# A two-layer hybrid block on one core: warm-up zeros in a place of their own, a fourth load buffer that comes in later, and a first block whose seven-product part starts four units later

## The chip, the cores and the metric

The kernel runs on one core of one Trainium2 chip. The metric is the time on the device in microseconds (us) of one execution; a kernel is run several times and the median counts. A profile is one further execution, recorded by the hardware profiler. Times inside it are counted from the start of its span. The engines are named as in the profile: PE multiplies matrices (PEld loads its weights), DVE and ACT work on vectors, POOL is hardly used, and SP issues the loads from memory (DMA). Each engine works through its own list of instructions in order. An instruction that waits holds up all that stand behind it on its engine.

## The reference

`x` has 256 rows of 2048 numbers in fp32. Two layers follow each other; each is a mixer and a gated feed-forward part (FFN), both added to the stream `h`, and a last norm ends it.

```python
def swiglu(hn, w_gate, w_up, w_down):
    return (jax.nn.silu(hn @ w_gate) * (hn @ w_up)) @ w_down

def reference(x, ...):
    h = x
    for layer in range(DEPTH):
        j = layer // 2
        if layer % 2 == 0:
            h = h + gdn_rglru_mixer(rmsnorm(h, ab_norm[j]), ab_w_in[j], ...)
        else:
            h = h + fox_moba_mixer(rmsnorm(h, cd_norm[j]), cd_w_in[j], ...)
        h = h + swiglu(rmsnorm(h, ffn_norm[layer]), ffn_w_gate[layer], ffn_w_up[layer], ffn_w_down[layer])
    return rmsnorm(h, final_norm)
```

The first mixer joins a gated delta rule and a linear recurrence, the second two kinds of attention. Most of the work is products of `hn` (256 x 2048) with weights: D_FF is 5632, so one FFN reads 3 x 2048 x 5632 weights.

## The kernel before

**Precision and units.** Every large product keeps fp32 by a split: a weight block `raw` of 128 x 1024 is loaded (`load`, L161), ACT rounds it to `whi` (L174), DVE forms `wlo` = raw - whi (L175), and PE makes three products: x-high with whi, x-high with wlo, x-low with whi (L366, L367, L368 in the FFN; L229 to L231 and L197 to L199 in the first mixer; L268 to L270 elsewhere). One such block is called a unit here. The activations stand transposed in `X`, high and low part. There are three buffers for `raw`, four for `whi`, three for `wlo`. Inside an FFN a fourth buffer `raw4` takes every fourth load; it lies in the pool `mx`, whose memory belonged to the mixer before, so that its first load must wait until the last readers and writers of that memory are done. The count of loads (`loads`) runs through the whole program.

**The start.** PE first multiplies a tile of zeros, `wz`, into `Pz` (L90), eleven times; each of these fp32 products is two rows of the trace. `wz` lies in a pool of its own that is closed at once, so the next pool to open gets its place: that is `xt`, the transposed input, in four quarters (L211). `first` then computes the first three weight columns (q, k, v of head 0): per quarter, ACT makes X high (L221) and DVE X low (L222) for four k, ACT and DVE split three half-size weight blocks (L225, L226), and PE makes 36 products of 256 columns, 144 in all. `x` in its untransposed form is loaded into `h` in four pieces (L893); ACT squares each (`junk`, L281), and DVE makes the row norms from the sums (`rstd`, L299 to L103), among the splits of the units of head 1 (`wstat`, L197).

**The FFN.** Gate and up weights are done in 11 blocks of 512 columns (`block`), for both of them and both row halves t. The 16 k-slices fall into four quarters m. Quarters 1 to 3 are plain: 12 units, named p0 to p11 here, of 12 products of 512 columns each, and each goes to the two banks of its matrix. Quarter 0 (2 x 2 sub-matrices b11, b12, b22, b21) is done by a scheme with seven products instead of eight, the generator `seven`: it loads b11, b12, b22, b21, forms the sums T1 = b11 + b12, T3 = b12 + b22, T2 = T1 + b22, T4 = T2 + b21 on DVE (`total`, L337), splits each sum (`thi` on ACT L340, `tlo` on DVE L341), and PE makes 6 products for each of seven steps. The sums of activations that it needs are made once, by `combine` (L349 to L354). A table of counts decides how many steps follow each plain unit:

```python
        lead, trail = 2, 3 if nd > 3 else 2
        gaps = max(len(plain) - lead - trail, 1)
...
            while k < len(sevens) and k < (j - lead + 2) * len(sevens) // gaps:
                next(sevens[k])
```

With these numbers one step follows each of the units p1 to p7. In the first block of an FFN `combine` runs ahead of p1 (`hooks[1]`), and `rstd` ahead of p8. The stream into the FFN comes from the mixer's last product: DVE adds it to h (L321), ACT squares it (`junk`), PE transposes it (`Pt`, L290), ACT and DVE write the last quarter of X (L291, L292).

**The order.** The program text gives what is done; a scheduler places the instructions on each engine, so a row of an engine's list need not stand where the text has it. The loads all go through SP's one list.

Of the kernel before, what the change touches and what calls it, by code (L numbers as in the profile page):

```python
# [4 lines left out]
F32, F32R, I32 = dt.float32, dt.float32r, dt.int32  # L5
AF = mybir.ActivationFunctionType
# [41 lines left out]
def body(tc, A, out):  # L48
    nc = tc.nc
    PE, S, V, G = nc.tensor, nc.scalar, nc.vector, nc.gpsimd  # L50
# [4 lines left out]
    cst = pool("cst", 1)  # L55
# [7 lines left out]
    loads, more = [0], []  # L63

    def phase(mixer):

        st = ExitStack()
        sub = lambda name, bufs: st.enter_context(tc.tile_pool(name=name, bufs=bufs))
        ogp.pool = sub("og" if mixer else "hid", 3 if mixer else 1)
        mx.pool = sub("mx" if mixer else "fx", 1)  # L70
        more[:] = [] if mixer else [1]
        return st

    def ms(shape, name):
        return msp.tile(shape, F32, tag="ms", name=name)
# [3 lines left out]
    X = res.tile([128, NK, 2, T], F32R, name="X", tag="X")  # L79
# [1 line left out]
    col = cst.tile([128, NCOL], F32, name="col")  # L81
    nc.sync.dma_start(col[:, 0:16], A["col"][:, 0:16])

    with tc.tile_pool(name="warm", bufs=1) as wp:
        wz = wp.tile([128, 256], F32, name="wz")
        V.memset(wz, 0.0)
        S.activation(wz[:, 0:1], wz[:, 1:2], AF.Copy)
        Pz = ms([128, 256], "Pz")
        for _ in range(11):
            PE.matmul(Pz, wz[:, 128:256], wz[:, 0:256], start=True, stop=True)  # L90
    tb = {n: tab[:, a:b] for n, (a, b) in TAB.items()}
    cl = {n: col[:, a:b] for n, (a, b) in COL.items()}

# [67 lines left out]
    def load(src):  # L161

        loads[0] += 1
        if more and loads[0] % 4 == 0:
            raw = mx.tile([128, 1024], F32, name="raw4", tag="raw4", bufs=1)
        else:
            raw = wr.tile([128, 1024], F32, name="raw")
        nc.sync.dma_start(raw, src)
        return raw
# [198 lines left out]
                PE.matmul(self.t, xl, hi[:, kk], start=False, stop=kk == 1 and self.i == self.n - 1)  # L368
            self.i += 1

    def block(src, x, comb, nd, hooks, tail=0):

# [41 lines left out]
            return [[c1, w5], [v, w7]]  # L416

        sevens = [s for m in comb for s in [seven(m)] for _ in range(7)]
        lead, trail = 2, 3 if nd > 3 else 2
        gaps = max(len(plain) - lead - trail, 1)  # L420
        held, e, k = [], None, 0
        for j, (i, u) in enumerate(plain):
# [14 lines left out]
            while k < len(sevens) and k < (j - lead + 2) * len(sevens) // gaps:  # L437
                next(sevens[k])
                k += 1
                if k == len(sevens):  # L440
                    e = ends()
        return [[y.t for y in f] for f in F], e

    def ffn(L, then, fin=None):

        gu, dn = A[f"gu{L}"], A[f"dn{L}"]
# [11 lines left out]
        b = 0  # L458
        for piece in (4, 4, 3):
            hid = ogp.tile([128, 16, 2, T], F32R, name="hid", tag="hid")  # L460
            for j in range(piece):
                hooks = {2: turn, 3: turn} if todo else {}
                if b == 0:
                    hooks[1] = lambda: cx.update({0: combine(X[:, 0:4])})
                    hooks[8] = rstd
                if j == 1:
                    hooks[5] = lambda: ch.update({0: combine(hid[:, 0:4])})
                F, e = block(lambda i, u: gu[b, u, i], lambda k: X[:, k], {0: lambda: cx[0]}, 4, hooks)
                a = [mx.tile([128, 512], F32, name=f"fa{t}", tag="fa", bufs=4) for t in range(2)]
                for t in range(2):  # L470
                    r = nrm["rs"][:, t:t + 1]
                    V.tensor_tensor(out=a[t], in0=F[t][0], in1=e[t][0], op=(ALU.add, ALU.subtract)[t])
                    S.activation(a[t], a[t], AF.Silu, scale=r)
                for t in range(2):
                    r = nrm["rs"][:, t:t + 1]
                    V.tensor_tensor(out=e[t][1], in0=F[t][1], in1=e[t][1], op=ALU.add)
                    V.scalar_tensor_tensor(out=a[t], in0=e[t][1], scalar=r, in1=a[t], op0=ALU.mult, op1=ALU.mult)
                    todo.append((hid, j, t, a[t]))
                b += 1
# [691 lines left out]
```

## Time and profile before

| | |
|---|---|
| time, median of 3 runs | 2288.99 us (2286.92 to 2289.01) |
| profiled execution, its own time | 2286.04 us |
| its span | 2284.2 us |
| PE busy | 2259.0 us, 99% of the span |
| DVE busy | 1805.0 us, 79% |
| ACT busy | 1205.9 us, 53% |
| moved from memory | 418.22 MB, 185 GB/s on average |
| mean granted clock of PE | 0.996 |

The profiled execution's own time is 1.8 us longer than its span, which begins with the first instruction and ends with the last. It lies 2.95 us under the median of the runs. The granted clock is a share of full speed, 1.00 for 2.4 GHz and 0.50 for 1.2 GHz. A busy PE is not a PE at its best: matmuls overlap, so what counts is how often one starts.

### The profile page before, as it was taken

The numbers are of one execution on the slowest core, as the hardware profiler recorded it, in microseconds if no ns is written. First come the engines' busy times: TensorE is split into PE (matmuls) and PEld (weight loads), VectorE is DVE, ScalarE is ACT, GpSimd is POOL, SyncE is SP. The second block draws the span as 40 slices with busy tenths as digits, with TensorE's granted clock in tenths as the row PEclk, the third lists the DMA queues.
The fourth block names the chain that finished last, engine by engine and source line by source line (L and its number), as shares of the span: only waits on it lengthen the run. The fifth ranks groups of instructions, "written<-read, shape, count | busy, mean of one in ns | idle before, by whom it ended". The sixth has DMA issues, their size and how long they took to land.

```text
span 2284.2 us, 31143 instructions
## 1 busy us (share of the span) xinstructions
PE 2259.0 (99%) x11620; PEld 1906.7 (83%) x11620; DVE 1805.0 (79%) x2655; ACT 1205.9 (53%) x1580; POOL 2.0 (0%) x6
## 2 busy tenths in 40 slices
PE   8999999999999999999999999999999999999997
PEld 8999888788888888888878888887888888888886
DVE  6898676688887888888976658857888788787888
ACT  6765654554554554454654444445554455554554
POOL 0000000000000000000000000000000000000000
PEclk9999999999999999999999999999999999999999
DMA  7444445566565566566554455455565565566564
GB/s 244 148 161 155 145 154 181 167 203 201 185 204 202 188 208 192 191 200 201 185 169 166 151 172 168 166 191 179 186 208 194 192 205 197 183 206 204 186 213 147
DMA packets 118647, 422.35 MB, mean 185 GB/s; under 512 B 13248, under 2 KB 14784, under 8 KB 118368
## 3 DMA queue, kind: packets, MB, share of 16 engines
q1 hardware_dynamic: 118208, 419.84, 55.4%
q8 instruction: 91, 1.49, 0.3%
q10 hardware_dynamic: 288, 0.52, 0.1%
q14 instruction: 60, 0.49, 0.1%
HBM read 418.22 MB, written 2.10 MB: 184 GB/s over the span
## 4 chain that ended last, share of the span: by engine, by line
PE 97%; DVE 1%; DMA 1%; ACT 1%; issue 0%; DVEq 0%; ACTq 0%; SPq 0%
PE F L366 17%; PE F L368 17%; PE F L367 17%; PE Pw L194 7%; PE Pw L199 6%; PE Px L268 5%; PE Px L270 4%; PE Px L269 4%; PE M L367 3%; PE M L368 3%; PE M L366 3%; PE Pw L197 2%; PE Pw L198 2%; PE Ph L453 1%; PE Psc L975 1%; DVE wlo L175 0%
## 5 line engine op out<-in xcount | busy, mean ns | idle before, releaser
L174 ACT CAST whi<-raw 128x1024 fp32r<-128x1024 f32 x744 | 779.9, 1052 | 889.1 <-PE F L368 424.1
L175 DVE TENSOR_TENSOR wlo<-raw,whi 128x1024 fp32r<-128x1024 f32 x744 | 906.1, 1222 | 329.5 <-PE F L367 141.9
L366 PE MATMUL F<-whi,X 128*128 128x512 f32 x1100 | 432.2, 393 | 5.6 <-ACT whi L174 5.6
L368 PE MATMUL F<-whi,X 128*128 128x512 f32 x1100 | 429.6, 391 | 0.0
L367 PE MATMUL F<-wlo,X 128*128 128x512 f32 x1100 | 429.4, 390 | 0.0
L199 PE MATMUL Pw<-X,wlo 128*128 128x256 f32 x1104 | 310.2, 281 | 0.0
L366 PEld LDWEIGHTS F<-whi,X 128*128 128x128 f32 x1100 | 206.8, 188 | 48.7 <-ACT whi L174 7.1
L368 PEld LDWEIGHTS F<-whi,X 128*128 128x128 f32 x1100 | 207.2, 188 | 43.6
L367 PEld LDWEIGHTS F<-wlo,X 128*128 128x128 f32 x1100 | 207.5, 189 | 42.1
L194 PE MATMUL Pw<-X,whi 128*128 128x512 f32 x640 | 230.2, 403 | 0.0
L366 PE MATMUL F<-whi,hid 128*128 128x512 f32 x536 | 209.9, 392 | 0.0
L199 PEld LDWEIGHTS Pw<-X,wlo 128*128 128x128 f32 x1104 | 209.5, 190 | 0.2
L368 PE MATMUL F<-whi,hid 128*128 128x512 f32 x536 | 208.7, 389 | 0.0
L367 PE MATMUL F<-wlo,hid 128*128 128x512 f32 x536 | 208.6, 389 | 0.0
L341 DVE TENSOR_TENSOR tlo<-T,thi 128x1024 fp32r<-128x1024 f32 x136 | 165.4, 1221 | 19.8 <-ACT thi L340 19.6
L340 ACT CAST thi<-T 128x1024 fp32r<-128x1024 f32 x136 | 142.7, 1049 | 28.8 <-PE M L368 14.9
L194 PEld LDWEIGHTS Pw<-X,whi 128*128 128x128 f32 x640 | 120.2, 188 | 29.4 <-issue 0.7
L197 PE MATMUL Pw<-X,whi 128*128 128x256 f32 x464 | 135.0, 291 | 0.0
L198 PE MATMUL Pw<-X,whi 128*128 128x256 f32 x464 | 131.4, 283 | 0.0
L368 PEld LDWEIGHTS F<-whi,hid 128*128 128x128 f32 x536 | 100.6, 188 | 21.0
L367 PEld LDWEIGHTS F<-wlo,hid 128*128 128x128 f32 x536 | 100.7, 188 | 20.6
L366 PEld LDWEIGHTS F<-whi,hid 128*128 128x128 f32 x536 | 100.6, 188 | 20.3
(372 smaller groups left out, 3241.9 us busy)
## 6 DMA issues: line engine op xcount, KB each, us to landing
raw<-in_gu SPq DMA_DIRECT2D x352, 512.0 KB, 4.1
raw<-in_dn SPq DMA_DIRECT2D x176, 512.0 KB, 4.2
raw<-in_w0w SPq DMA_DIRECT2D x74, 512.0 KB, 3.6
raw<-in_wo SPq DMA_DIRECT2D x64, 512.0 KB, 3.5
raw<-in_w1w SPq DMA_DIRECT2D x64, 512.0 KB, 3.5
raw<-in_w1x SPq DMA_DIRECT2D x32, 512.0 KB, 3.5
raw<-in_w0x SPq DMA_DIRECT2D x16, 512.0 KB, 3.5
raw<-in_w0w SPq DMA_DIRECT2D x12, 256.0 KB, 5.3
```

What stands on the lines that cost most here:

```text
L174: S.copy(hi, raw)
L175: V.tensor_sub(lo, raw, hi.bitcast(F32))
L194: PE.matmul(P.rearrange("p a b -> p (a b)"), hi[:, kk], X[:, k].rearrange("p a b -> p (a b)"), start=k == 0, stop=False)
L197: PE.matmul(P[:, 0], hi[:, kk], X[:, k, 0], start=k == 0, stop=False)
L198: PE.matmul(P[:, 0], hi[:, kk], X[:, k, 1], start=False, stop=False)
L199: PE.matmul(P[:, 0], lo[:, kk], X[:, k, 0], start=False, stop=k == NK - 1)
L268: PE.matmul(Ps[t], x[:, 0, ts], hi[:, kk], start=k == 0, stop=False)
L340: S.copy(hi, t)
L341: V.tensor_sub(lo, t, hi.bitcast(F32))
L366: PE.matmul(self.t, xh, hi[:, kk], start=self.i == kk == 0, stop=False)
L367: PE.matmul(self.t, xh, lo[:, kk], start=False, stop=False)
L368: PE.matmul(self.t, xl, hi[:, kk], start=False, stop=kk == 1 and self.i == self.n - 1)
```

## The change

Three things are changed. The zeros `wz` get a place in the pool of constants, which nobody else uses, and they are multiplied six times instead of eleven. `loads` is set to -12 whenever a stage (mixer or FFN) begins, and `raw4` is used only at positive multiples of four, that is from the 16th load of a stage on. In the first block of each FFN `combine` runs ahead of p4 instead of p1, and `lead` is 5 instead of 2: with 4 gaps in place of 7, one step of the seven follows p4, two follow p5, two p6 and two p7.

```diff
@@ -69,6 +69,7 @@
         ogp.pool = sub("og" if mixer else "hid", 3 if mixer else 1)
         mx.pool = sub("mx" if mixer else "fx", 1)
         more[:] = [] if mixer else [1]
+        loads[0] = -12
         return st
 
     def ms(shape, name):
@@ -81,13 +82,12 @@
     col = cst.tile([128, NCOL], F32, name="col")
     nc.sync.dma_start(col[:, 0:16], A["col"][:, 0:16])
 
-    with tc.tile_pool(name="warm", bufs=1) as wp:
-        wz = wp.tile([128, 256], F32, name="wz")
-        V.memset(wz, 0.0)
-        S.activation(wz[:, 0:1], wz[:, 1:2], AF.Copy)
-        Pz = ms([128, 256], "Pz")
-        for _ in range(11):
-            PE.matmul(Pz, wz[:, 128:256], wz[:, 0:256], start=True, stop=True)
+    wz = cst.tile([128, 256], F32, name="wz")
+    V.memset(wz, 0.0)
+    S.activation(wz[:, 0:1], wz[:, 1:2], AF.Copy)
+    Pz = ms([128, 256], "Pz")
+    for _ in range(6):
+        PE.matmul(Pz, wz[:, 128:256], wz[:, 0:256], start=True, stop=True)
     tb = {n: tab[:, a:b] for n, (a, b) in TAB.items()}
     cl = {n: col[:, a:b] for n, (a, b) in COL.items()}
 
@@ -161,7 +161,7 @@
     def load(src):
 
         loads[0] += 1
-        if more and loads[0] % 4 == 0:
+        if more and loads[0] > 0 and loads[0] % 4 == 0:
             raw = mx.tile([128, 1024], F32, name="raw4", tag="raw4", bufs=1)
         else:
             raw = wr.tile([128, 1024], F32, name="raw")
@@ -368,7 +368,7 @@
-    def block(src, x, comb, nd, hooks, tail=0):
+    def block(src, x, comb, nd, hooks, tail=0, lead=2):
@@ -416,7 +416,7 @@
         sevens = [s for m in comb for s in [seven(m)] for _ in range(7)]
-        lead, trail = 2, 3 if nd > 3 else 2
+        trail = 3 if nd > 3 else 2
         gaps = max(len(plain) - lead - trail, 1)
@@ -461,11 +461,11 @@
                 if b == 0:
-                    hooks[1] = lambda: cx.update({0: combine(X[:, 0:4])})
+                    hooks[4] = lambda: cx.update({0: combine(X[:, 0:4])})
                     hooks[8] = rstd
-                F, e = block(lambda i, u: gu[b, u, i], lambda k: X[:, k], {0: lambda: cx[0]}, 4, hooks)
+                F, e = block(lambda i, u: gu[b, u, i], lambda k: X[:, k], {0: lambda: cx[0]}, 4, hooks, lead=2 if b else 5)
```

What the change does to the engines' lists is shown at three places. First SP, at the start of the program, with what each load waits for in brackets (names with DMAHW are earlier loads); before:

```order
L82 DMA col<-in_col 128x16
L216 DMA raw<-in_w0w 128x512 x3
L218 DMA tab<-in_tab 128x152
L219 DMA col<-in_col 128x233
L216 DMA raw<-in_w0w 128x512 x2
L216 DMA raw<-in_w0w 128x512 [waits DMAHW0_49]
L893 DMA h<-in_x 128x2x512 [waits DMAHW1_49]
L211 DMA xt<-in_xt 128x1024 [waits DMAHW2_49,PE_49,Activation_49]
```

And now:

```order
L83 DMA col<-in_col 128x16
L211 DMA xt<-in_xt 128x1024
L216 DMA raw<-in_w0w 128x512 x3
L218 DMA tab<-in_tab 128x152
L219 DMA col<-in_col 128x233
L211 DMA xt<-in_xt 128x1024
L216 DMA raw<-in_w0w 128x512 [waits DMAHW0_49]
L216 DMA raw<-in_w0w 128x512 [waits DMAHW1_49]
L216 DMA raw<-in_w0w 128x512 [waits DMAHW2_49]
L211 DMA xt<-in_xt 128x1024 [waits DMAHW3_49]
L211 DMA xt<-in_xt 128x1024 [waits DMAHW4_49]
```

The first quarter of `xt` moved to second place and waits for nothing; the first piece of h went behind all quarters and weight halves of `first`.

Second SP again, at the beginning of the first FFN (the second FFN has the same rows under other numbers). Before, 5147 is p0's block, 5175 p1's, 5193 b11, 5223 b12, 5255 b22:

```order
L168 DMA raw_5147<-in_gu0 128x1024 [waits DMAHW0_49,DVE_49,Activation_49]
L168 DMA raw_5193<-in_gu0 128x1024 [waits DMAHW1_49,DVE_49]
L168 DMA raw_5205<-in_gu0 128x1024 [waits DMAHW2_49,DVE_49]
L168 DMA raw_5223<-in_gu0 128x1024 [waits DMAHW3_49,DVE_49]
L168 DMA raw4_5175<-in_gu0 128x1024 [waits PE_49,Activation_49,Pool_49]
L168 DMA raw4_5237<-in_gu0 128x1024 [waits DMAHW7_49,DVE_49]
L168 DMA raw_5255<-in_gu0 128x1024 [waits DMAHW4_49,DVE_49]
```

Now 5138, 5156, 5174, 5192 and 5220 are p0 to p4, 5238 is b11, 5250 p5, 5268 b12, 5282 b22, 5294 p6, 5336 p7, 5354 b21, and 5457 is p11, the 16th load:

```order
L168 DMA raw_5138<-in_gu0 128x1024 [waits DMAHW0_49,DVE_49,Activation_49]
L168 DMA raw_5156<-in_gu0 128x1024 [waits DMAHW1_49,DVE_49]
L168 DMA raw_5174<-in_gu0 128x1024 [waits DMAHW2_49,DVE_49]
L168 DMA raw_5192<-in_gu0 128x1024 [waits DMAHW3_49,DVE_49]
L168 DMA raw_5220<-in_gu0 128x1024 [waits DMAHW4_49,DVE_49,Activation_49]
L168 DMA raw_5238<-in_gu0 128x1024 [waits DMAHW5_49,DVE_49]
L168 DMA raw4_5457<-in_gu0 128x1024 [waits PE_49,Activation_49,Pool_49]
L168 DMA raw_5250<-in_gu0 128x1024 [waits DMAHW6_49,DVE_49]
L168 DMA raw_5268<-in_gu0 128x1024 [waits DMAHW7_49,DVE_49]
L168 DMA raw_5282<-in_gu0 128x1024 [waits DMAHW2_49,DVE_49]
L168 DMA raw_5294<-in_gu0 128x1024 [waits DMAHW0_49,DVE_49]
```

The load that waits for the mixer's memory moved from fifth place, where p1's block hung on it, to seventh, where p11's does.

Third DVE in the same block, from T1 on; before:

```order
L337 TENSOR_TENSOR T1_5225<-raw_5193,raw_5223 128x1024
L352 TENSOR_TENSOR cc4_5166<-cf_5165,cc4_5166 128x256
L175 TENSOR_TENSOR wlo_5178<-raw4_5175,whi_5177 128x1024
L352 TENSOR_TENSOR cc4_5166<-cf_5165,cc4_5166 128x256
L175 TENSOR_TENSOR wlo_5196<-raw_5193,whi_5195 128x1024
L175 TENSOR_TENSOR wlo_5208<-raw_5205,whi_5207 128x1024
L354 TENSOR_TENSOR comb_5167<-cc4_5166,comb_5167 128x1024
L341 TENSOR_TENSOR tlo_5228<-T1_5225,thi_5227 128x1024
L175 TENSOR_TENSOR wlo_5240<-raw4_5237,whi_5239 128x1024
L337 TENSOR_TENSOR T3_5285<-raw_5223,raw_5255 128x1024
```

Now:

```order
L101 TENSOR_TENSOR rt_5388<-rs_5389 128x2
L102 SCALAR_TENSOR_TENSOR rt_5388<-rt_5388,rx_5387 128x2
L175 TENSOR_TENSOR wlo_5253<-raw_5250,whi_5252 128x1024
L354 TENSOR_TENSOR comb_5212<-cc4_5211,comb_5212 128x1024
L337 TENSOR_TENSOR T1_5270<-raw_5238,raw_5268 128x1024
L103 SCALAR_TENSOR_TENSOR rs_5389<-rt_5388,rs_5389 128x2
L101 TENSOR_TENSOR rt_5388<-rs_5389 128x2
L102 SCALAR_TENSOR_TENSOR rt_5388<-rt_5388,rx_5387 128x2
L103 SCALAR_TENSOR_TENSOR rs_5389<-rt_5388,rs_5389 128x2
L337 TENSOR_TENSOR T3_5312<-raw_5268,raw_5282 128x1024
L341 TENSOR_TENSOR tlo_5273<-T1_5270,thi_5272 128x1024
```

T1 moved from the start of the block to behind p5's split, the small operations of `rstd` (L299 to L103) came up from behind the seven steps, and T3 now stands ahead of T1's `tlo`, where before it stood behind it.

## Rows read from the trace of the kernel before

**Rows 1.** The page: the span, and PE's busy time.

```profile
span 2284.2 us, 31143 instructions
PE 2259.0 (99%) x11620; PEld 1906.7 (83%) x11620; DVE 1805.0 (79%) x2655; ACT 1205.9 (53%) x1580; POOL 2.0 (0%) x6
```

**Rows 2.** PE's waits: in total us, how often, longest us.

```profile
PE F L366 <- ACT whi L174: 5.6, 4, 2.5
PE Pw L229 <- ACT X L221: 4.5, 1, 4.5
```

**Rows 3.** Timeline of the start: start us, length us, engine, [idle before, releaser].

```profile
1.19 1.36 SPq L216 DMA_DIRECT2D raw<-in_w0w  x3
2.28 7.86 PE L90 MATMUL Pz<-wz 128*128 128x256 f32 x22 [2.28 <-ACT wz L87]
10.23 1.29 SPq L211 DMA_DIRECT2D xt<-in_xt  x3
14.04 4.91 ACT L221 ACTIVATE X<-xt,col 128x256 fp32r<-128x256 f32 x12 [2.45 <-DMA xt<-in_xt]
14.60 0.56 PE L229 MATMUL Pw<-X,whi 128*128 128x256 f32 x2 [4.46 <-ACT X L221]
...
24.82 2.50 DVE L226 TENSOR_TENSOR wlo<-raw,whi 128x512 fp32r<-128x512 f32 x4
...
33.65 0.28 PE L197 MATMUL Pw<-X,whi 128*128 128x256 f32 x1
```

**Rows 4.** SP's waits: the load of xt.

```profile
SPq L211 <- PE Pz L90: 4.5, 1, 4.5
```

**Rows 5.** Windows at the start, PE alone, the last of all engines: busy, clock, DMA, GB/s.

```profile
2.28:7.55 5.27, 5.27 (x12) 1.00 0.96 301
14.60:18.30 3.70, 3.70 (x17) 0.54 0.99 361
18.30:33.64 15.34, 15.34 (x129) 1.00 0.89 319
15.00:20.00 5.00, 5.00 (x30) 4.88 (x30) 4.47 (x12) 4.46 (x11) 0.00 (x0) 0.67 0.99 367
```

**Rows 6.** Windows of PE in FFN blocks: the first, second, first again, half clock.

```profile
444.22:492.64 48.42, 45.36 (x195) 0.96 0.57 186
492.64:535.79 43.15, 43.15 (x195) 1.00 0.60 196
1559.14:1607.77 48.63, 45.67 (x195) 0.96 0.56 186
451.80:455.20 3.40, 3.03 (x8) 0.50 0.59 175
```

**Rows 7.** The chain that ended last, where the FFNs begin.

```profile
444.46 1.41 ACT junk L281 x4
445.93 3.45 DMA raw<-in_gu
...
1560.81 3.37 DMA raw<-in_gu
```

**Rows 8.** PE's timeline in the first FFN block.

```profile
450.57 0.73 PE L366 MATMUL F<-whi,X 128*128 128x512 f32 x2 [2.47 <-ACT whi L174]
```

**Rows 9.** DVE's timeline in the first FFN block.

```profile
467.54 2.35 DVE L175 TENSOR_TENSOR wlo<-raw,whi 128x1024 fp32r<-128x1024 f32 x2
469.81 1.22 DVE L337 TENSOR_TENSOR T<-T,raw 128x1024 f32<-128x1024 f32 x1
470.94 0.16 DVE L98 TENSOR_SCALAR rs<-rt 128x2 int32<-128x2 int32 x1
471.14 0.16 DVE L101 TENSOR_TENSOR rt<-rs 128x2 f32<-128x2 f32 x1
```

**Rows 10.** DVE's timeline where the first norms are made.

```profile
29.56 0.16 DVE L299 TENSOR_REDUCE rx<-ssp 128x2 f32<-128x8 f32 x1 [2.23 <-ACT junk L281]
35.92 1.22 DVE L175 TENSOR_TENSOR wlo<-raw,whi 128x1024 fp32r<-128x1024 f32 x1
```

## The prediction

> **What bounds the kernel now.** I read the page first. PE is busy for 2259.0 of the 2284.2 us [rows 1], so only stretches in which PE idles or runs slowly can give time back. PE's waits then name the places: 4.5 us before its first real product, and 5.6 us in four waits for a `whi` in the FFNs [rows 2]. The other engines wait for PE almost everywhere else, so what they do matters only where PE waits for them.
>
> The timeline of the start shows the first place. PE multiplies zeros from 2.28 for 7.86 us, and only then, at 10.23, does SP issue the loads of xt; the first real product starts at 14.60 [rows 3]. SP's waits say why: the load of xt waited 4.5 us for Pz [rows 4], because it lies where the zeros lay. After the idle stretch PE's clock is half: 17 products take 3.70 us, while the 129 that follow take 15.34 us, 0.119 each [rows 5]. Product 145 of the real work starts at 33.65 [rows 3], and from there on PE runs without a gap to the FFN.
>
> The second place is the first block of each FFN. The second block takes 43.15 us, the first 48.42 and in the second FFN 48.63, with as many products [rows 6]. So each first block loses 5.27 and 5.48 us. The chain shows the cause: the mixer's last ACT work on h, then a load of 3.45 us (3.37 in the second FFN) that could not be issued before [rows 7]. PE stood 2.47 us [rows 8], and the clock fell to half for the stretch 451.80 to 455.20 [rows 6].
>
> **The change, part by part: the start.** xt is now SP's second load; that place is issued at 1.19 [rows 3]. From issue to the first X took 3.8 us before (10.23 to 14.04), so the first X starts at about 5.0. Four X on ACT at 0.41 each (4.91 / 12), then the first half-size `whi` at about 0.6, end at 7.2. Six zero products are twelve rows, which took until 7.55 [rows 5]; so the first real product starts at about 7.6, and its `wlo` is there about 8.2. I add 0.6 us for this and for a last stretch at half clock, and 144 times 0.119 = 17.1: the 144 end at 25.3 instead of 33.65, a gain of 8.35.
>
> Does the feed hold this pace? A quarter is 36 products, 4.3 us of PE. DVE needs four X at 0.41 and three `wlo` at 0.63 (2.50 / 4 [rows 3]), 3.5 us; ACT is alike. The loads of a quarter are 0.52 + 3 x 0.26 = 1.31 MB, 3.6 us at the 367 GB/s of [rows 5]. All three stay under PE, with some 0.7 us per quarter to spare.
>
> What is late next is h. All of its four pieces stand behind `first`'s loads, so they land at about the time of before: 2.1 MB of h, 1.0 MB of two units and 5.4 MB ahead of them make 8.5 MB, 23 us at 367 GB/s, after about 3 us until the first lands: 26.2. Two squares of 0.7 later, at 27.6, DVE starts the norms (29.56 before [rows 10]); about 14 small steps that depend on each other, 0.20 each [rows 9], and two of 128 columns end at 30.8. On DVE the third `wlo` of head 1 stands behind them and is ready at 32.0. PE wants it after two units of 24 products, 25.3 + 5.8, and one small product of the norms: 31.5. I take a wait of 0.5, which leaves **-7.8 us**. Bounds: no wait, -8.4; or the norms come as late as before, the third `wlo` at 35.92 + 1.22 = 37.1 [rows 10], a wait of 5.6, and only -2.7. I stay near the first, since the loads before h lose the stretch in which the queue waited for Pz.
>
> The five zero products that are gone lay ahead of an idle stretch before; now they would lie ahead of real work, and the 7.6 above counts that. The place for wz and the order inside the mixer I cost at nothing: PE is the engine waited for there. Blocks after the first keep four load buffers in rotation, only beginning elsewhere in it, so their loads wait for the same uses as before: nothing either, and 2 us of disturbance per FFN would be the bound if this were wrong.
>
> **The first FFN blocks.** Four plain units no longer hang on the late load: p0 to p4 have their blocks in the three ordinary buffers. The 5.27 and 5.48 us go away. But the seven steps now come compressed and with three buffers. I count from the block's first product. PE, without waits: a unit of 12 products is 2.72 us (0.227 each: 43.15 less 0.9 for eight transposes, over 186), a step of six 1.36; with 0.8 for the transposes p0 ends at 3.5, p1 6.3, p2 9.0, p3 11.7, p4 14.4, step b11 15.8, p5 18.5, and then the six products of T1 start.
>
> DVE: p5's `wlo` needs the place of p3's, free at 11.7, and stands behind eight small steps of `rstd`, which run until about 12.1. A DVE operation of 128 x 1024 starts 1.14 us after the one before and lasts 1.22 [rows 9]. So p5's `wlo` is done at 13.2, the last part of `combine` at 14.4, T1 at 15.6. Only then can b22 be loaded, as its buffer is the one that T1 read b11 from: 15.6 + 3.45 [rows 7] = 19.05. T3 needs b22 and stands ahead of T1's `tlo` on DVE: T3 until 20.2, `tlo` until 21.4. PE wanted it at 18.7: **a wait of 2.7 us**.
>
> The same repeats with b21, whose buffer is b22's, last read by T2. After T3 DVE does T1's `tlo`, two `wlo`, T3's `tlo` and T2, 5 x 1.14, until 25.9; the load lands at 29.4; T4 until 30.6, and behind it T2's `tlo` until 31.8. PE has 35 products from 21.4 on, 7.95 us, and stands at 29.4: **a second wait of 2.45 us**. The 72 products that are left take 16.35, and the block ends at 48.2. Against 48.42 and 48.63 that is -0.2 and -0.4: the stall is not removed but moved.
>
> Half clock changes this little. If the first wait brings it, as 2.47 us did [rows 8], eight products start in 3.40 us [rows 6] where fifteen would, 1.6 us lost; PE then comes 1.6 later to the second wait, which shrinks as much, since DVE's chain sets its end. Bounds for a block: neither wait, -5.3; both, with half clock after the second instead, +1.4. The prices of DVE and of the load are rows of the same kind in the same stage, so I take the sum.
>
> [...]
>
> **Sum.** -7.8 - 0.2 - 0.4 = -8.4 us. The profiled execution's own time, 2286.04, becomes 2277.6; it lay 2.95 under the median, so I put the same difference on the median: 2288.99 - 8.4 = **2280.6 us**.
>
> **Rivals.** (B) *The waits of the first block do not appear, or half of them.* For it: T1 needs only be 2.7 us earlier, or DVE might find `rstd` done in pauses. Against it: T3 stands ahead of `tlo` in DVE's list, and the buffer rule holds whatever the clock does. It gives -7.8 - 10.7 = -18.5, 2270.5; with half the waits about 2275.5.
>
> (C) *h takes the gain of the start back.* The norms come as late as before, a wait of 5.6 where I have 0.5; or the two FFN blocks end 1.4 later by half clock after the second wait. The first gives 2288.99 - 2.7 - 0.6 = 2285.7, the second 2288.99 - 7.8 + 2.8 = 2284.
>
> (D) *PE's clock does not rise in `first`* and the kernel ends slower. The place is the first 144 products; before, eleven zero products ran ahead of an idle stretch, and half clock lasted for 17 products after it. If fewer zeros and pauses between the first products keep the clock at half, 144 products take 144 x 3.70 / 17 = 31.3 us, from 7.6 to 38.9 instead of 33.65: +5.3 - 0.6 = +4.7, 2293.7. Each us at half clock costs half a us, so the start gives nothing back once about 16 us run so. Against it: before, real products brought the clock up after 17 of them [rows 5].
>
> On (D) the Trainium skill, TensorE: Matmul & The Clock Gate, "What's actually happening", says that "the default state is throttled, and activity releases the throttle". By that rule five zeros fewer speak for (D), the earlier real products against it; the trace agrees as far as the half clock behind the idle stretch goes.
>
> **How the numbers follow.** The forecast, within about 3 us either way, has 0.55; (B) 0.20, (C) 0.17, (D) 0.06, and 0.02 is left for something slower still. The range from 2274 to 2287 takes in the half of (B) and all of (C). About 0.2% (4.6 us) is what a measurement of this kernel can tell from no change. The forecast is faster by more than that except for its slow edge; (B) is faster; (C) is the same or just at the bound; (D) is slower or at the bound. So faster 0.75, same 0.19, slower 0.06.
>
> **What would show it.** In the profile after: no wait of SP's xt load for Pz, a first real product near 7.6, and head 1's first product near 25.3, at full clock from about 8 on. In the FFNs no wait for `whi` at the block's start, but two waits for `tlo`, at L367 of an M bank, some 18.7 and 29.4 us into the first block, and a block length of about 48. First blocks of 43 to 46 us would make (B) right; PE waiting for the third `wlo` of head 1 for several us, (C); a granted clock of 0.5 beyond the first 10 us, (D).

## The result, and the profile of the changed kernel

The changed kernel takes **2272.97 us** (median of 6 runs, 2272.34 to 2276.77). The kernel before, run beside it, takes 2287.14 (6 runs, 2285.41 to 2289.01). The ratio is 0.9941 with a 95% interval of 0.9931 to 0.9952, about 14.2 us less. The forecast was 8.4 us less and 2280.6, with a range down to 2274.0. The sign was right. The gain was larger than every case but rival (B), and the median lies 1.0 us below the range.

The page, its span and PE's busy time, for comparison with [rows 1]:

```profile
span 2270.7 us, 31138 instructions
PE 2252.9 (99%) x11610; PEld 1901.3 (84%) x11610; DVE 1804.5 (79%) x2655; ACT 1201.8 (53%) x1579; POOL 2.0 (0%) x6
```

The span is 13.5 us shorter. This profiled execution took 2272.64 us in all, close to its median, while that of before lay 1.1 under its median of six; the rest of the 14.2 is there. PE's waits, in total us, how often, longest us, which answer to [rows 2]:

```profile
PE M L367 <- DVE tlo L341: 1.7, 4, 0.5
PE Pw L199 <- DVE wlo L175: 1.1, 2, 0.8
PE Prb L311 <- PE Pw L199: 0.8, 1, 0.8
PE Pw L197 <- ACT whi L174: 0.6, 1, 0.6
```

Beside these stands PE's first wait of 2.3 us for `wz`, which the kernel before has too. Both rows of [rows 2] are gone: PE no longer waits 5.6 us for a `whi` in the FFNs nor 4.5 us for X. New are three rows at the start (`Pw` L199, `Prb`, `Pw` L197). The four waits for a `tlo` are the places where the forecast had two waits of 2.7 and 2.45 us per block; the longest is 0.5.

The timeline of the start (start us, length us, engine, and in brackets the idle time before and what ended it), for [rows 3]:

```profile
1.19 0.42 SPq L211 DMA_DIRECT2D xt<-in_xt  x1
2.28 5.49 PE L90 MATMUL Pz<-wz 128*128 128x256 f32 x12 [2.28 <-ACT wz L87]
5.42 1.70 ACT L221 ACTIVATE X<-xt,col 128x256 fp32r<-128x256 f32 x4 [3.19 <-DMA xt<-in_xt]
7.69 0.49 PE L229 MATMUL Pw<-X,whi 128*128 128x256 f32 x1
...
12.57 2.96 SPq L216 DMA_DIRECT2D raw<-in_w0w  x6
...
24.98 0.28 PE L229 MATMUL Pw<-X,whi 128*128 128x256 f32 x1
...
26.09 0.39 PE L197 MATMUL Pw<-X,whi 128*128 128x256 f32 x1 [0.59 <-ACT whi L174]
27.35 0.39 PE L199 MATMUL Pw<-X,wlo 128*128 128x256 f32 x1 [0.76 <-DVE wlo L175]
33.95 0.46 PE L311 MATMUL Prb<-dg,tab 128*128 128x128 f32 x2 [0.83 <-PE Pw L199]
35.24 0.39 PE L199 MATMUL Pw<-X,wlo 128*128 128x256 f32 x1 [0.36 <-DVE wlo L175]
```

`first` went as forecast: its first product at 7.69 (forecast 7.6), its last ones right behind 24.98, where the kernel before stood at 33.3. Head 1's first product comes at 26.09 (25.3) instead of 33.65. But then PE waits four times, 0.59 + 0.76 + 0.83 + 0.36 = 2.54 us, where the forecast had one wait of 0.5. At the FFN's first product 4.75 us are left of the 7.56 (439.47 against 444.22).

The windows of the first block of the first FFN and of the second (busy time of PE, PEld, DVE, ACT, POOL, then clock, DMA share, GB/s):

```profile
439.47:484.42 44.95, 44.12 (x196) 35.38 (x194) 38.99 (x55) 26.54 (x32) 0.00 (x0) 1.00 0.62 198
1550.63:1595.29 44.66, 43.79 (x195) 35.46 (x194) 39.03 (x55) 26.54 (x32) 0.00 (x0) 1.00 0.63 200
```

The first blocks last 44.95 and 44.66 us, 3.5 and 4.0 less than in [rows 6], and nothing in them runs at half clock. The forecast was 48.2. So 13.5 us of span are 4.75 at the start, 3.47 and 3.97 in the two first blocks, and 1.3 in the rest: 0.35 and 0.7 in the later blocks of the two FFNs, 0.3 behind the last product, and nothing in the second mixer.

Why the waits for `tlo` are short is seen on DVE and SP in the first block (the T at 453.95 is T1, at 456.49 T3, at 462.99 T2; the `wlo` at 451.67 is p5's, at 460.71 p6's):

```profile
451.67 1.23 DVE L175 TENSOR_TENSOR wlo<-raw,whi 128x1024 fp32r<-128x1024 f32 x1
453.95 1.22 DVE L337 TENSOR_TENSOR T<-raw 128x1024 f32<-128x1024 f32 x1
456.49 1.22 DVE L337 TENSOR_TENSOR T<-raw 128x1024 f32<-128x1024 f32 x1 [0.66 <-DMA raw<-in_gu]
457.63 1.22 DVE L341 TENSOR_TENSOR tlo<-T,thi 128x1024 fp32r<-128x1024 f32 x1
460.71 1.23 DVE L175 TENSOR_TENSOR wlo<-raw,whi 128x1024 fp32r<-128x1024 f32 x1 [0.72 <-ACT whi L174]
462.99 1.22 DVE L337 TENSOR_TENSOR T<-T,raw 128x1024 f32<-128x1024 f32 x1
...
452.93 0.33 SPq L168 DMA_DIRECT2D raw<-in_gu  x1
455.20 0.33 SPq L168 DMA_DIRECT2D raw<-in_gu  x1
461.96 0.33 SPq L168 DMA_DIRECT2D raw<-in_gu  x1
```

T1 ends at 455.17, 15.7 us into the block, as forecast (15.6). But b22 is not loaded behind it. Its load is issued at 452.93, right behind p5's `wlo` (451.67 + 1.23 = 452.90), into the place that p5's block has just left. The load that waits for T1 (455.20) is p6's. T3 starts at 456.49 and T1's `tlo` ends at 458.85, where the forecast had 439.47 + 21.4 = 460.9. b21 is issued at 461.96, behind p6's `wlo` (460.71 + 1.23 = 461.94), not behind T2, which ends at 464.21.

### The profile page after: what moved, and what is told of

Same layout as the page of the kernel before. It is cut to its first block, busy times and chain, and to the rows that moved or that the text cites. A ratio compares the mean times of both kernels' runs of the same rounds, so it can differ in the third digit from the quotient of the medians.

```text
span 2270.7 us, 31138 instructions
## 1 busy us (share of the span) xinstructions
PE 2252.9 (99%) x11610; PEld 1901.3 (84%) x11610; DVE 1804.5 (79%) x2655; ACT 1201.8 (53%) x1579; POOL 2.0 (0%) x6
## 4 chain that ended last, share of the span: by engine, by line
PE 94%; DVE 2%; DMA 2%; ACT 0%; issue 0%; SPq 0%; DVEq 0%; ACTq 0%
PE F L366 17%; PE F L368 17%; PE F L367 17%; PE Pw L194 7%; PE Pw L199 6%; PE Px L268 5%; PE Px L270 4%; PE Px L269 4%; PE M L367 2%; PE M L368 2%; PE M L366 2%; PE Pw L197 2%; PE Pw L198 2%; DMA raw<-in_gu 1%; PE Ph L453 1%; DVE wlo L175 1%
## 5 line engine op out<-in xcount | busy, mean ns | idle before, releaser
L199 PE MATMUL Pw<-X,wlo 128*128 128x256 f32 x1104 | 310.5, 281 | 1.1 <-DVE wlo L175 1.1
L368 PEld LDWEIGHTS F<-whi,X 128*128 128x128 f32 x1100 | 206.5, 188 | 43.1
L199 PEld LDWEIGHTS Pw<-X,wlo 128*128 128x128 f32 x1104 | 209.5, 190 | 1.7 <-DVE wlo L175 1.5
L197 PE MATMUL Pw<-X,whi 128*128 128x256 f32 x464 | 135.2, 291 | 0.6 <-ACT whi L174 0.6
```

The source lines that it names most:

```text
L197: PE.matmul(P[:, 0], hi[:, kk], X[:, k, 0], start=k == 0, stop=False)
L199: PE.matmul(P[:, 0], lo[:, kk], X[:, k, 0], start=False, stop=k == NK - 1)
```

## The experiments

For each kernel: median, ratio to the kernel before with its 95% interval, the time of the FFN's first product, and the lengths of the first blocks of the two FFNs, read from first product to first product in one profiled execution. Each ratio, and each gain named below, is against the kernel before as it ran beside that experiment: 2286.89 us for e1 to e4, 2287.26 for e5, e6, e8 and lead 4, 2287.43 for e9 to e11 and lead 3.

| kernel | median us | ratio | FFN's first product | first blocks |
|---|---|---|---|---|
| before | 2287.14 | | 444.22 | 48.42, 48.63 |
| changed | 2272.97 | 0.9941 (0.9931 to 0.9952) | 439.47 | 44.95, 44.66 |
| e1: zeros alone | 2283.61 | 0.9986 (0.9978 to 0.9995) | 438.81 | 49.71, 49.38 |
| e2: raw4 alone | 2280.61 | 0.9974 (0.9964 to 0.9983) | 444.71 | 46.45, 46.05 |
| e3: lead alone | 2283.35 | 0.9985 (0.9976 to 0.9994) | 443.58 | 48.03, 46.36 |
| e4: changed, eleven zeros | 2272.59 | 0.9941 (0.9927 to 0.9954) | 440.57 | 44.19, 44.45 |
| e5: changed, forecast's buffers | 2277.94 | 0.9956 (0.9943 to 0.9968) | 440.30 | 45.92, 45.63 |
| e6: changed, half of h earlier | 2273.83 | 0.9941 (0.9928 to 0.9953) | 441.26 | 44.94, 44.46 |
| e7: changed, lead 4 | 2271.63 | 0.9927 (0.9914 to 0.9941) | 441.90 | 43.31, 43.56 |
| e7: changed, lead 3 | 2272.28 | 0.9935 (0.9923 to 0.9948) | 442.20 | 43.93, 43.97 |
| e8: changed, one zero | 2271.76 | 0.9931 (0.9919 to 0.9944) | 440.26 | 44.36, 44.55 |
| e9: lead 4 and one zero | 2272.07 | 0.9931 (0.9918 to 0.9945) | 442.17 | 43.49, 43.37 |
| e10: changed, little of h | 2270.47 | 0.9930 (0.9918 to 0.9943) | 441.45 | 44.88, 44.72 |
| e11: changed, again | 2273.37 | 0.9940 (0.9928 to 0.9953) | 441.03 | 44.77, 44.73 |

**The three parts alone.** e1 takes the `wz` lines of the diff, e2 the two lines on `loads`, e3 the lines on `lead` and `hooks`; each leaves the rest as before.

> Only the zeros' own place and their six products; raw4 and the seven as in the kernel before. Theory (the account of the two traces): the start is worth what the traces differ by at the FFN's first product, 444.22 - 439.47 = 4.75 us, and nothing else changes: 2287.1 - 4.7 = 2282.4 us; head 1's first product at 26.1, the first FFN block 48.4 us long with its stall of about 3.1 us. Rival 1 (the prediction's term): -7.8 us, 2279.3. Rival 2 (the start's gain is tied to the FFN part, and is lost at the late load of raw4): under 2 us, above 2285.

> Only the fourth buffer from a stage's 16th load on; start and lead as in the kernel before. Theory (the late load is nearly all of the stall): no wait for a whi in the first blocks, their lengths fall from 48.4 and 48.6 to about 45, with waits for a tlo under 1 us, together -7 to -9 us: about 2279. Rival 1 (the seven must move too): with one step behind each of p1 to p7 and three buffers PE waits 2 us or more in each block for a tlo or for comb; blocks of 46.5 to 48, -1 to -4 us in all, 2283 to 2286. Rival 2 (the prediction's buffer rule): two waits of about 2.5 us per block, 2286 to 2287.

> Only the first block's seven four units later (combine ahead of p4, lead 5); start and fourth buffer as in the kernel before. Theory (the late load is the cause): p1's block is still in raw4 and issued as the fifth load, behind the mixer's last readers, so PE stands for its whi as before, 2 to 2.5 us and half clock behind it; blocks of 47.5 to 49, total between -1 and +1: 2286 to 2288. Rival (the early work on DVE, combine and T1, is what holds PE up): the stall goes, blocks of about 45, -7 us: 2280.

e1 gained 3.3 us where 4.7 were expected. The start did its part, 5.4 us at the FFN's first product, but the first blocks became longer, 49.71 and 49.38. The stall is the same as before, the half clock behind it lasts twice as long. The windows of e1 at half clock:

```profile
445.70:452.40 6.70, 6.49 (x15) 4.42 (x14) 6.28 (x7) 4.32 (x5) 0.00 (x0) 0.50 0.62 219
1561.90:1568.60 6.70, 6.53 (x14) 4.59 (x15) 6.35 (x8) 4.81 (x5) 0.00 (x0) 0.50 0.53 173
```

15 and 14 products start in 6.70 us, where 30 would at full clock. In the kernel before the same waits (2.47 us and 2.30) brought 3.40 us of it [rows 6].

e2 gained 6.3 us, between its theory and its first rival. The stall for `whi` at the block's start is gone without the later seven, so the late load was its cause. Its blocks are 1.4 to 1.5 us longer than the changed kernel's: that is what the later seven are worth. (e2's profiled execution is the slowest of its nine, 2283.86; it waits 1.81 us for a `tlo` at 2222.88, far behind the first blocks, with 3.3 us at half clock after it.) PE's waits in the first block of e2 (line numbers one higher):

```profile
PE F L367 <- ACT whi L175: 0.4, 1, 0.4
PE F L368 <- DVE wlo L176: 0.4, 1, 0.4
PE M L367 <- ACT comb L354: 0.2, 1, 0.2
```

e3 gained 3.5 us where about 0 was expected. The stall is there as the theory says, 2.55 us in the first FFN and 2.40 in the second. But in the second no half clock follows it. PE's row there, and under it the windows behind both stalls:

```profile
1564.45 0.73 PE L366 MATMUL F<-whi,X 128*128 128x512 f32 x2 [2.40 <-ACT whi L174]
```

```profile
450.90:454.20 3.30, 3.24 (x8) 2.56 (x9) 3.30 (x4) 2.85 (x4) 0.00 (x0) 0.50 0.51 159
1564.45:1571.00 6.55, 6.33 (x27) 4.93 (x28) 5.84 (x6) 4.57 (x5) 0.00 (x0) 1.00 0.55 178
```

Eight products in 3.30 us behind the first stall, 27 in 6.55 behind the second. The three medians sum to -13.1 us, all parts together gave -14.2: so much of a sum as can be asked where the half clock behind one stall costs from nothing to 3.4 us.

**The buffers of the seven (e5).** In the first block b22 and b21 go where the forecast put them:

```diff
-            b22 = load(src(1, 2 * m + 1))
+            b22 = b11 if strict else load(src(1, 2 * m + 1))
+            if strict:
+                nc.sync.dma_start(b22, src(1, 2 * m + 1))
...
-            b21 = load(src(0, 2 * m + 1))
+            b21 = b22 if strict else load(src(0, 2 * m + 1))
+            if strict:
+                nc.sync.dma_start(b21, src(0, 2 * m + 1))
```

> The changed kernel, but in the first block of each FFN b22 is loaded into the place of b11, and b21 into the place of b22, as the prediction took for granted. The output is the same. The scheduler now puts T1's tlo ahead of T3 on DVE. Theory (the step that failed is the rule on which buffer b22 and b21 get: with the rule in force the waits come): b22's load is issued right behind T1, 3 to 4 us later than in the changed kernel, and b21's right behind T2; PE waits 1 to 3 us per block for b22's or b21's parts, blocks of 46 to 48, +2 to +6 us against the changed kernel: 2275 to 2279. Rival (the buffer did not matter, since DVE's list and the time of PE's need were mis-sized): waits as now, under 1 us a block, 2272.5 to 2274.

The theory held in sign: 2277.94, 5.0 us more than the changed kernel, though the intervals of the two ratios overlap. The total lies in its range, the blocks just below its 46 to 48. SP, DVE and PE of e5 in the first block (L401 is b22's load, L411 b21's):

```profile
454.78 1.22 DVE L337 TENSOR_TENSOR T<-raw 128x1024 f32<-128x1024 f32 x1
456.02 0.33 SPq L401 DMA_DIRECT2D raw<-in_gu  x1
460.28 1.22 DVE L337 TENSOR_TENSOR T<-raw 128x1024 f32<-128x1024 f32 x1 [1.95 <-DMA raw<-in_gu]
461.38 0.50 PE L366 MATMUL F<-whi,comb 128*128 128x512 f32 x1 [0.84 <-ACT whi L174]
462.33 0.73 PE L366 MATMUL F<-whi,X 128*128 128x512 f32 x2 [0.45 <-ACT whi L174]
```

b22's load now follows T1, and T3 starts 20.0 us into the block (460.28 - 440.30), where the changed kernel has 17.0 and the forecast had 19.05. PE waits 0.84 + 0.45 us. The blocks are 1.0 us longer than the changed kernel's, not the 3.3 that the forecast had, because with this edit the scheduler puts T1's `tlo` ahead of T3 on DVE, so the late b22 no longer holds up T1's products. The spans of the two profiles differ by 5.9 us. 1.9 of them lie in the first blocks, 0.8 in the start, 1.1 between the first block and the second FFN, and 2.0 at the end of the second FFN (1.4 us of waits for `tlo` there). So most of what e5 lost is not shown to come from the two buffers.

**When the seven start (e7, e9).** Lead and hook are one or two lower:

```diff
-                    hooks[4] = lambda: cx.update({0: combine(X[:, 0:4])})
+                    hooks[3] = lambda: cx.update({0: combine(X[:, 0:4])})
-                F, e = block(..., hooks, lead=2 if b else 5)
+                F, e = block(..., hooks, lead=2 if b else 4)
```

> The changed kernel with lead 4 and combine ahead of p3, one unit earlier. Theory (what PE still waits for in the first blocks, 0.83 and 0.87 us for tlo, is DVE's chain from combine to T4, 2.7 us short of nothing): T1 is formed a unit earlier, the waits for tlo vanish, blocks of 43.9 to 44.2, -1 to -1.5 us in all: 2271.5 to 2272. Rival (combine and T1 then meet the splits of the first plain units, which are late because the loads start late at an FFN): PE waits for a wlo or comb instead, blocks of 45 to 46.5, +0.5 to +3: 2273.5 to 2276.

> The changed kernel with lead 3 and combine ahead of p2. Theory (with the steps early, combine and the sums meet the first splits, which start late at an FFN since the loads do; lead 2 with a late fourth buffer gave blocks of 46.5 and 46.1, lead 4 43.3 and 43.6): between the two, 44 to 45.5, about the changed kernel's time, 2272 to 2274. Rival (earlier is better until the X's last quarter is there): 43.1 to 43.5, 2271.

With lead 4 the blocks are 43.31 and 43.56, with lead 3 43.93 and 43.97. The windows of e7 with lead 4:

```profile
441.90:485.21 43.31, 43.31 (x195) 35.54 (x194) 38.98 (x55) 26.54 (x32) 0.00 (x0) 1.00 0.68 206
1551.74:1595.30 43.56, 43.49 (x195) 35.54 (x194) 38.84 (x55) 26.44 (x32) 0.00 (x0) 1.00 0.67 205
```

PE is busy for all of the first block and waits 0.07 us in the second: there is nothing left to gain there. The theory for lead 4 had 43.9 to 44.2, its rival 45 and more; the rival fell. With lead 3 the theory was about right (43.9 where it had 44 and more), and its rival, which had 43.1 to 43.5, fell. The four blocks with lead 4 (here and in e9) take 43.3 to 43.6, the twelve with lead 5 and free buffers 44.2 to 44.95. So lead 4 saves some 1.2 us a block by the traces; in the timed runs its median is 1.3 us under the changed kernel's, and the intervals overlap.

**The start: zeros (e4, e8, e9).** The number in `range(6)` becomes 11 or 1; e9 has one zero and lead 4.

> The changed kernel with eleven zero products instead of six, in their own place; the order of all else is the same. Ten rows more take 7.86 - 5.49 = 2.4 us, so the first real product starts at 10.1 and head 1's first at about 28.4. Theory (after first() PE is bound by the loads of head 1's blocks and by the norms, which don't wait for the zeros): PE's waits of 0.59, 0.76, 0.83 and 0.36 us shrink by about as much as the zeros add; the kernel is 0 to 0.6 us slower than the changed one: 2273 to 2273.6. Rival (PE's time is paid in full, since the splits' pace follows PE): +2.4 us, 2275.4.

> The changed kernel with one zero product instead of six: two rows, which end at about 3.3; then PE idles until the first real product at 7.7. Theory (an idle stretch of 4.4 us ahead of real work brings half clock, as the 4.46 us did in the kernel before): granted clock 0.5 for 3.4 to 6.8 us somewhere before 16 us, 1.7 to 3.4 us lost in first(), of which the later waits for loads and norms give back about half, as with the eleven zeros (1.1 of 1.8 us were left at the FFN): +0.5 to +1.7, 2273.5 to 2274.7. Rival (the clock stays low through first(), the prediction's case D): first() takes up to 31 us, +5 or more, 2278 or above. Rival 2 (no zeros are needed): within 0.3 us of the changed kernel.

> The changed kernel with lead 4, combine ahead of p3, and one zero product instead of six: the two edits that cost nothing or gained. Theory (the two do not touch each other): first blocks of 43.3 to 43.6 us, start as in the changed kernel within its spread from execution to execution (439 to 442 at the FFN's first product), -1.5 to -2.5 us against the changed kernel: 2270.5 to 2271.5. Rival (the first block's length hangs on when it starts, and the gain of lead 4 was chance): 2272.5 to 2273.5.

Eleven zeros: 2272.59. One: 2271.76. Six: 2272.97 and 2273.37. The number of zeros makes no difference that these runs can tell; the rival that had the eleven paid in full fell. With eleven the first real product comes at 9.49, 1.8 us later (not 2.4: the first 12 rows of zeros take until about 7.4, the last 10 only until 9.4), the FFN's first product 1.1 us later than in the changed kernel's first profile, and 0.5 earlier than in its second. With one, PE idles 4.08 us ahead of the first product and then starts 14 products in 3.12 us, where the next 29 take 3.20:

```profile
7.58 0.58 PE L229 MATMUL Pw<-X,whi 128*128 128x256 f32 x1 [4.08 <-ACT whi L225]
```

```profile
7.58:10.70 3.12, 3.12 (x14) 3.10 (x15) 2.62 (x6) 2.31 (x6) 0.00 (x0) 1.00 1.03 407
10.80:14.00 3.20, 3.20 (x29) 3.20 (x28) 3.18 (x8) 3.16 (x8) 0.00 (x0) 1.00 0.88 331
```

(The clock column shows 1.00 in the first of the two windows, but 0.22 us per product is the pace of half clock; the trace's first record of the clock, at 10.755, says full, and it has none before that.) About 1.5 us are lost there, where e8's theory had 1.7 to 3.4. Against the changed kernel's profile 0.8 of it is left at head 1's first product (26.88 instead of 26.09) and at the FFN's (440.26 instead of 439.47): the later waits gave back about half, as the theory had it, but a spread of 3.4 us between kernels with one start (see below) hides so little. The total, 2271.76, lies under its 2273.5 to 2274.7. The clock did rise, so e8's first rival fell; whether its second is right these runs do not tell. e9 did not add two gains: 2272.07 is 1.3 us under the changed kernel on the same chip, between its theory and its rival. Its blocks are as its theory had them, but its start is not: 27 products take the 5.90 us from 7.40 to 13.30, where the next 23 take 2.60, and from 37.3 to 40.6 the granted clock is 0.50 once more.

**The start: h (e6, e10).** In e6 the first two pieces of h are issued ahead of the weight halves on which SP stands until 12.57; in e10 each early load of h brings 64 of 512 columns:

```diff
             nc.sync.dma_start(xt[:, ks], A["xt"][:, ks])
+            if q == 2:
+                for g in range(2):
+                    nc.sync.dma_start(h[:, :, g * 512:(g + 1) * 512], A["x"][:, :, g * 512:(g + 1) * 512])
```

```diff
-                        nc.sync.dma_start(h[:, :, g * 512:(g + 1) * 512], A["x"][:, :, g * 512:(g + 1) * 512])
-                        sumsq(g)
+                        nc.sync.dma_start(h[:, :, g * 512:g * 512 + 64], A["x"][:, :, g * 512:g * 512 + 64])
+                        for t in range(2):
+                            j = mx.tile([128, 512], F32, name="junk", tag="t2", bufs=4)
+                            S.activation(j[:, 0:64], h[:, t, g * 512:g * 512 + 64], AF.Square, accum_out=ssp[:, t, g:g + 1])
```

> The changed kernel with the first two pieces of h issued behind the third quarter of xt, ahead of the weight halves on which SP stands from 8.07 to 12.57 us until DVE has read the places they go to. Theory (the start's lost 3.6 us come from the queue that runs dry in that pause: the loads of head 1's blocks and of h, behind it, come late): the DMA share between 12.5 and 15 us rises from 0.79 to about 1, all of h is there at 27 to 28 instead of 29.5, the waits behind first() fall from 2.5 us to under 1.5, total -1 to -2: 2271 to 2272. Rival (the pause is harmless; the loads as such are the bound, and 1 MB of h ahead of the weights makes first() wait): PE waits within first() for the third quarter, 0 to +1.5 us, 2273 to 2274.5.

> The changed kernel, but each early load of h brings only 64 of its 512 columns, and the squares are formed of these alone; the other columns are loaded during head 2. It leaves out most of the sum behind the first norms, so its output is not the reference's. 0.26 MB instead of 2.1 MB stand between first() and head 1's blocks. Theory (what eats the start's gain behind first() is that h's pieces stand ahead of head 1's blocks in the queue and the norms behind h): the wait for head 1's first whi vanishes, the norms are there before PE wants them, of the 3.5 us lost behind first() 2 to 3 come back; the FFN's first product at 437 to 438 instead of 439.5 to 442, total 2270 to 2271. Rival (the loss is the three raw buffers and the splits of ACT and DVE, not the bytes): at most 0.7 us, 2272 to 2273.

> The changed kernel once more on this chip, as the measure for the three others: 2272 to 2274 us; its start differs from execution to execution by as much as the others' with the same start have shown, the FFN's first product between 438.8 and 441.9.

e6's theory fell. The pause in the queue did fill, as the windows of the changed kernel and then of e6 show (last columns DMA share and GB/s):

```profile
12.50:15.00 2.50, 2.50 (x23) 2.50 (x22) 2.50 (x7) 2.45 (x7) 0.00 (x0) 1.00 0.79 267
15.00:20.00 5.00, 5.00 (x44) 5.00 (x43) 4.77 (x10) 4.01 (x9) 0.00 (x0) 1.00 0.97 292
```

```profile
12.50:15.00 2.50, 2.50 (x22) 2.50 (x22) 2.50 (x6) 2.45 (x7) 0.00 (x0) 1.00 1.04 383
15.00:20.00 5.00, 4.07 (x32) 3.66 (x31) 2.43 (x5) 4.38 (x14) 0.00 (x0) 1.00 1.05 377
```

And PE's waits in e6's timeline (line numbers of `first` three higher):

```profile
17.52 0.39 PE L232 MATMUL Pw<-X,whi 128*128 128x256 f32 x1 [0.92 <-ACT whi L228]
27.59 0.39 PE L197 MATMUL Pw<-X,whi 128*128 128x256 f32 x1 [0.91 <-ACT whi L174]
29.36 0.55 PE L199 MATMUL Pw<-X,wlo 128*128 128x256 f32 x1 [1.26 <-DVE wlo L175]
```

But the weights of the third quarter now come later, PE waits 0.92 us for them at 17.5, the three buffers come free later, head 1's blocks are issued at 22.10 instead of 19.67, and PE waits for their parts. The norms no longer hold it up: they begin at 26.58 instead of 30.92. The waits changed places, half clock followed the last of them (29.5 to 32.8), and the time is the same.

e10 took the bytes away, and the waits with them: of the four only one is left, 1.21 us at 27.06 (`Pw` L199). The fifth block behind `first`, which starts with product 33 of L197, starts at 38.80 instead of 40.86 (changed) and 42.41 (e11). Its median is 2.9 us under e11's on the same chip, though the intervals overlap. The profiled execution itself lost this again at 77.79, where PE waited 2.19 us for the gates behind the moved loads and then ran at half clock (79.60 to 82.90); it took 2274.31, the longest of the five runs. The squares are shorter too in e10 (0.24 us each instead of 0.62), so bytes and ACT's work are not told apart.

## Why the prediction was wrong, point by point

**The start, mechanism.** Right. xt waits for nothing, `first` begins at 7.69 and keeps its pace of 0.12 us per product to the end. SP's wait for Pz [rows 4] is gone.

**The start, size: the term -7.8 was 3.1 us too large in the changed kernel's profile.** The step that failed is that h's pieces "make 8.5 MB, 23 us at 367 GB/s, after about 3 us until the first lands: 26.2". The last piece landed at 29.5, and the norms began at 30.92 instead of 27.6 (29.56 before, [rows 10]); the square of the last piece on ACT, and the norms' first step on DVE:

```profile
29.55 0.63 ACT L281 ACTIVATE junk<-h 128x512 f32<-128x512 f32 x1 [0.66 <-DMA h<-in_x]
30.92 0.16 DVE L299 TENSOR_REDUCE rx<-ssp 128x2 f32<-128x8 f32 x1 [2.36 <-ACT junk L281]
```

The rate of 367 GB/s was that of a full queue; here SP stood from 8.07 until 12.57 with the second half's weights in hand, since the places they go to were still being filled and read, and the rate was 267 and 292 GB/s up to 20 us. The chain behind it was sized well: from the norms' start to the third `wlo` 4.3 us were measured (30.92 to 35.18), 4.4 forecast. I had also left out that head 1's own first blocks stand behind two pieces of h: 0.59 and 0.76 us. So rival (C) named the mechanism, with a part of its size: the norms came even later than before, but PE's two waits around them are 0.83 and 0.36 us, not 5.6. In e6 the norms began ahead of the forecast's 27.6 and nothing was gained, since the weights came late in their place: what was mis-sized is rather the time for all these loads than h's place among them. e10, with little of h's bytes and work, comes 2.1 us earlier to the fifth block (38.80 instead of 40.86).

What the start is worth is not one number: the FFN's first product came between 438.8 and 442.2 in the profiles of six kernels with the same start (changed, e1, e5, both e7, e11), and at 443.6 to 444.7 in three with the old one. So the term was 2.4 to 5.8 us too large over these six. In e11 the gain is 3.2 us. There head 1's first wait is 1.54 us, and PE runs at half clock behind it (e11's timeline, then a window):

```profile
27.57 0.39 PE L197 MATMUL Pw<-X,whi 128*128 128x256 f32 x1 [1.54 <-ACT whi L174]
```

```profile
30.10:33.40 3.30, 3.30 (x18) 3.30 (x17) 0.81 (x7) 2.04 (x7) 0.00 (x0) 0.50 1.03 402
```

The same is seen in e5 and both e7: head 1's first wait is 0.86, 1.42 and 2.18 us, a granted clock of 0.50 follows for 3.4 us somewhere between 27.7 and 33.2, and the FFN begins at 440.3 to 442.2. In the changed kernel's profile and in e1 that wait is 0.59 and 0.38 us, no half clock follows, and the FFN begins at 439.47 and 438.81. At half clock a product starts every 0.21 us, where 0.12 is full pace, so such a stretch loses some 1.5 us: the clock makes a part of this spread.

**The five zeros.** The forecast counted them as time won. In the timed runs of e4 and e8 they are worth nothing that can be told. By the profiles 1.1 of the 1.8 us of e4's later start are left at the FFN's first product, less than the spread just named.

**The first blocks: the terms -0.2 and -0.4 were -3.5 and -4.0.** The stall went as forecast. The step that failed is "Only then can b22 be loaded, as its buffer is the one that T1 read b11 from", and its twin for b21. I took the three places to be handed out in turn. They are not: a load gets the place that is free first, and p5's `wlo` frees one 2.3 us ahead of T1, p6's one 2.3 us ahead of T2's end (461.94 against 464.21). SP's rows at 452.93 and 461.96 show it, and the changed kernel's order of loads, which stood ahead of the forecast, has b22 ahead of p6. Everything up to T1 was right to some 0.2 us. With the rule in force and T3 still ahead of `tlo`, the load would be issued at 455.2, T3 would start near 458.7 and `tlo` end near 461.0, 2.4 us behind PE's need at 458.57, close to the 2.7 forecast. e5 put the rule in force: b22 came late as forecast, but the scheduler changed DVE's order, so only 1.0 us of the 3.4 per block is shown to hang on the buffer; the rest is argued from the rows.

Rival (B) was the right one for the FFNs. Its argument against itself, that "the buffer rule holds whatever the clock does", was the error. Its size was too large by 1.8 and 1.5 us per block, of which 0.83 and 0.87 are waits for a `tlo`; with lead 4 nearly all of it goes.

**Blocks after the first.** Costed at nothing with 2 us as the bound; they gave 0.35 and 0.7. The wait for a `tlo` near 2213 ranged from nothing (e6) to 1.4 us (e4) over kernels whose order there is the same, so they are not shown to come from the change.

**(D), the clock.** The trace's first record of the clock, at 7.95, is full, and from 8.43 on a product starts every 0.12 us, so (D) did not occur. The rule of the Trainium skill, TensorE: Matmul & The Clock Gate, "What's actually happening", that activity releases the throttle, agrees with e8: after one zero and 4.08 us idle, 14 products at half pace, then full.

**The load's price.** b22's load took from 452.93 until T3 started at 456.49, 3.6 us, near the 3.45 of [rows 7]. The Trainium skill, DMA: Bandwidth & Descriptors, "Anatomy of one DMA", fits a load that GpSimd issues by 2.0 us plus its bytes at 436 GB/s, an estimate of 3.2 us for 512 KB. SP issues the loads here, so the rows decide.

**Errors of both signs.** In the profiles compared, the start was taken 3.1 us too good, the first blocks 6.8 us too bad, and 1.3 us lie in small places. The forecast also stood on a median of three runs, 2288.99, where six gave 2287.14: 1.9 of the 7.6 us between 2280.6 and 2272.97 are that. With the base of six the range would have reached down to 2272.2 and taken the median in. That the range was missed by only 1.0 us is luck all the same: two wrong terms cancel in part.

## What to carry to other kernels

Before a wait is put on a buffer, read in the order of loads and in the releasers which place a load really gets: with tiles handed out as they come free, the late reader of one buffer delays somebody else's load. A stall that is removed at the start of a stage is worth what the next resource leaves of it; count the bytes that must land before the next work and the time in which the issuing queue itself stands, not a mean rate. A part that fills idle time ahead of a load-bound stretch (the zeros) may not show in the total at all: one, six and eleven gave 2271.8, 2273.0 and 2272.6 us, no difference that these runs can tell.

## What the runs showed of the hardware that was not expected

The same stall of PE has no fixed price in clock. Waits of 2.3 to 2.55 us at the start of an FFN were followed by 3.4 us at half clock in both FFNs before, by 6.7 in both of e1, by 3.4 and by none in the two of e3. So a stall of this length cost between nothing and 3.4 us besides itself. The Trainium skill, TensorE: Matmul & The Clock Gate, "What's actually happening", says that the number of slow matmuls at a kernel's start differs from run to run; these rows show such a spread in the middle of a kernel. At a kernel's start e8 and e9 show it, which have the same zeros: full pace began near 10.8 us in one and near 13.4 in the other.

The DMA rate behind the pause at 12.57 us stayed at 267 and 292 GB/s for some 7 us, at a busy share of 0.79 and 0.97, and in e11 at 238 and 257, where e6, whose queue had not run dry, had 383 and 377. Why busy engines moved less there stays open.
